# Context FFN in three passes with its own banks beside the later quarters, and a modulation on VectorE that the scheduler may place

## The chip, the cores and the metric

The kernel runs on one core of one Trainium2 chip. The metric is the device time of one execution in microseconds (us), taken over several runs. Profiles show one execution each: TensorE appears as PE (its weight loads as PEld), VectorE as DVE, ScalarE as ACT, GpSimd as POOL, SyncE, which issues nearly all DMAs, as SP.

## What is computed

Two blocks follow each other on 256 tokens of width 1024, all in float32. The first block has a layer with a token mix (a bidirectional RWKV-7 recurrence beside a Hyena long convolution), a convolved FFN and a gated embedding, and a layer with neighbourhood attention. The second block is a two-layer network over two streams, `x` and a context `ctx`, whose norms are modulated by vectors made from `c` and `c_ctx`. What matters here is that the first half FFN of the context in the second block does not depend on the first block at all:

```
z   = rmsnorm(x, mix_norm) @ mix_w_in                      # 3328 columns
x   = x + concat(rwkv7_bidir(z[:1664]), hyena_bidir(z[1664:])) @ mix_w_out
x   = x + conv_ffn(x) ; x = x + ple(x) ; x = x + na(x) ; ...
...
mc  = split(silu(c_ctx) @ w_mod[0] + b_mod[0], 9)           # and ml from c
ctx = ctx + 0.5 * mc[2] * swiglu(rms_norm(ctx, g) * (1 + mc[1]) + mc[0], wg, wu, wd)   # D_FF = 2816
```

## The kernel before

Activations lie feature by feature: 8 tiles of 128 features by 256 tokens. Weights come from memory as tiles of 128 rows by up to 1024 columns, one DMA each. The exact products are made in one of two ways. `plain` (L397) gives TensorE the float32 tiles as they are; the trace shows two records for each such product. `gemm` (L368) first splits both operands into a rounded high part and a rest, with a cast on ScalarE (L362) and a subtraction on VectorE or GpSimd (L363), and then runs three passes, high by high, high by rest, rest by high (L371 to L373).

The program is written as one sequence, and a scheduler then sets the order of each engine's instructions for good. It may move an instruction of one part ahead of another part unless the instruction is pinned with `keep_in_program_order`, or the buffers do not allow it: a tile can only be written when the last user of its buffer is done. Each engine then works through its list in order, and so does SP with the DMAs.

`mix` (L839) is the first layer's token mix. The recurrence is cut into four quarters of two heads each (`Recurrence.prepare`, L1587, and `Recurrence.solve`, L1663). A quarter prepares its operands (products L1606, sums, exponentials, many VectorE steps), forms a triangular system (L1678), inverts it in six levels (products L1705, each followed by VectorE steps L1719, L1724, L1725), walks through four chunks (L1739, L1743, L1750), and writes its output (L1769 to L1782). Nothing in a quarter's chain can be reordered, so the scheduler puts other TensorE work between its steps: the projections by `w_in0` (`project`), the Hyena filters and the convolution (`filters`, `hyena`), the output product (`out0`), and the context's work. Quarters use the PSUM tags `a` and `b` in turn, three banks each, and all other work shares the two banks of tag `fill`.

The context's work in `mix` has three parts. `mod_first` (L1019) makes 24 modulation tiles for layer 0 on TensorE: 48 products of two columns by 512 (L1030), with transposes behind them. `norm_ctx` (L956) norms the context. `ctx_ffn` (L967) then runs the FFN in eight groups of three hidden tiles (`FILL`); its first four groups (`CUT`) run in `mix` by `plain` (up products L400 from `xc`, down products L1006), the others later by `gemm` in the gaps of the next layers, in the pool `own`, with GpSimd doing the subtractions.

PSUM is one pool per stage. The pool of `mix` closes at its end, and the next stage (`conv_ffn` of layer 0, here ffn0) opens another one with tags `mm`, `aux` and `fill`; without the pool option `reuse_waits="tile"` the new pool waits for the old one as a whole. Weights of `plain` land in the pool `wha` (tags `wh` and `wl`, two buffers each) through `room` (L392).

Later modulation tiles are made by `mod_until` (L1054): for each tile a DMA of 512 KB, and on VectorE a multiplication with the broadcast vector and a sum (L1077), one per stream or one with help of GpSimd (`aid`), all pinned to the program's order.

Of the kernel before, what the change touches and what calls it, by code (L numbers as in the profile page):

```python
# [153 lines left out]
def layout(inp):  # L154
# [17 lines left out]
    for l in range(2):  # L172
# [30 lines left out]
    a["ccf"] = np.ascontiguousarray(a["cc"].reshape(2, KT, P).transpose(2, 1, 0))  # L203
    a["w_modk"] = np.ascontiguousarray(
        g["w_mod_2"][0][:, :3072].reshape(4, 2, P, 6, 512).transpose(3, 0, 2, 1, 4).reshape(24, P, 1024))
# [70 lines left out]
class Net:  # L276
# [98 lines left out]
    def plain_tiles(self, name, todo):  # L375

        arr = self.ap[name]
        i = 0
        while i < len(todo):
            t, k0, kn = todo[i]  # L380
            n = kn * P
            m = 1
            while i + m < len(todo) and (m + 1) * n <= 1024 and todo[i + m] == (t + m, k0, kn):
                m += 1
            raw = self.room()
            src = arr[t : t + m, :, k0 * P : k0 * P + n].rearrange("t p n -> p t n")
            self.nc.sync.dma_start(raw[:, : m * n].rearrange("p (t n) -> p t n", t=m), src)
            for j in range(m):
                yield t + j, raw[:, j * n : (j + 1) * n]
            i += m  # L390

    def room(self):  # L392

        self.whi += 1
        return self.t(self.wha, [P, 1024], ("wh", "wl")[self.whi % 2])

    def plain(self, out, w, kt, x):  # L397

        for k in range(kt):
            self.nc.tensor.matmul(out, w[:, k * P : (k + 1) * P], x[:, k], start=k == 0, stop=k == kt - 1)  # L400
# [89 lines left out]
    def sq_add(self, m, s=0):  # L490

        nc = self.nc
        x = self.t(self.nrm, [P, T], f"ss{s}", bufs=1) if m == 0 else self.t(self.nrm, [P, T], "xt")
# [6 lines left out]
        else:  # L500
            self.sl[s].append(x)

# [8 lines left out]
    def norm1(self, pool, gname, tag="xn"):  # L511
# [5 lines left out]
        for k in range(KT):  # L517
            x = self.t(self.nrm, [P, T], "xt")
# [320 lines left out]
    def mix(self, ef):  # L839
# [4 lines left out]
        with ExitStack() as es:  # L844
            pool = self.pool(es, "mix")
            y = self.t(pool, [P, 4, T], "y")
            cs = self.t(pool, [P, KT, 2], "cs")
            nc.sync.dma_start(cs, self.ap["ccf"])
            self.tc.keep_in_program_order(nc.scalar.activation(cs, cs, AF.Silu))
            xp = self.pool(ef, "xc", side="right")  # L850
            xc = Parts([self.t(xp, [P, T], "xc", bufs=KT + 1) for _ in range(KT)])
            fp = self.pool(es, "fill", side="right")
            with ExitStack() as e2:
# [7 lines left out]
                with ExitStack() as e3:  # L861
# [3 lines left out]
                    with ExitStack() as e4:  # L865
# [6 lines left out]
                        self.tag = self.aux = "fill"  # L872
# [38 lines left out]
                        with ExitStack() as e5:  # L911
                            yp = self.pool(e5, "hyf")
                            self.tag = self.aux = "fill"
# [3 lines left out]
                            self.tag = self.aux = "fill"  # L917
# [5 lines left out]
                        project([7, 3, 11])  # L923
                        self.tag = self.aux = "fill"
                        self.mod_first(pool, cs)
                        self.norm_ctx(xc)
                        project([14 + 4 * j + q for q in range(4) for j in range(3)])
                    for j in range(2, 4):
                        solve(j, prepare(j))
                        if j == 2:  # L930
                            self.tag = self.aux = "fill"
                            self.hyena(x0, sv, kr, ki, hn)
                self.tag = self.aux = "fill"
# [5 lines left out]
        fp = self.pool(ef, "fill2", side="right")  # L939
        xh, xl = self.t(fp, [P, KT, T], "xnh", F32R), []  # L940
        for k in range(KT):
# [861 lines left out]
```

## Time and profile before

| what | value |
|---|---|
| three runs, median (lowest to highest) | 2967.49 us (2966.17 to 2968.52) |
| profiled execution, its own time | 2961.21 us |
| its span | 2959.4 us |
| granted TensorE clock, mean over the span | 0.964 |
| busy: PE, PEld, DVE, ACT, POOL | 96%, 83%, 63%, 40%, 13% |
| first product of ffn0 (L409) | 604.54 us after the start |

A matmul's record is drawn from its start to its modelled end and overlaps the next ones, so a busy TensorE can be one that waits between short products. What a product costs in a row of equal ones is the step from one start to the next. A line of the code can be a helper's, so a group is known by its line and its tiles together.

### The profile page before, as it was taken

How to read it: one execution, taken by the hardware profiler on the slowest of the kernel's cores; microseconds unless marked ns; L12 is line 12 of the kernel's file. 1: busy time of each engine (PE TensorE's matmuls, PEld its weight loads, DVE VectorE, ACT ScalarE, POOL GpSimd, SP SyncE). 2: the span in 40 equal slices, each digit the busy share in tenths (PEclk: the TensorE clock that was granted, in tenths of full speed). 3: DMA queues.
4: the chain of work that ended last, by engine and by line, in shares of the span. 5: the costliest groups of instructions: out<-in, count | busy, mean ns of one | idle time of the engine just before them, and what ended most of it. 6: DMA issues, size and time to landing. Idle time of an engine off the chain costs nothing.

```text
span 2959.4 us, 48347 instructions
## 1 busy us (share of the span) xinstructions
PE 2834.2 (96%) x19346; PEld 2452.0 (83%) x19346; DVE 1877.3 (63%) x3408; ACT 1175.0 (40%) x2065; POOL 385.9 (13%) x254
## 2 busy tenths in 40 slices
PE   7999999999989989988999999999999999999999
PEld 5756777889989889988998758888888888896899
DVE  5424632288977768886773584777765555558555
ACT  3202200065555545555554463322233222355443
POOL 0000000032252421122220101000010000102100
PEclk7998988999999999999999999999999999999999
DMA  4142123466545536645751203555544444221464
GB/s 133 51 144 95 52 80 119 130 226 206 199 166 168 148 115 215 212 147 197 227 179 57 91 1 107 171 178 178 170 150 130 152 132 144 91 92 57 148 194 150
DMA packets 146914, 414.81 MB, mean 140 GB/s; under 512 B 31153, under 2 KB 51266, under 8 KB 145922
## 3 DMA queue, kind: packets, MB, share of 16 engines
q1 hardware_dynamic: 145970, 406.48, 42.9%
q0 software_dynamic: 720, 5.24, 0.4%
q8 instruction: 153, 2.51, 0.3%
q14 instruction: 71, 0.58, 0.1%
HBM read 410.62 MB, written 1.05 MB: 139 GB/s over the span
## 4 chain that ended last, share of the span: by engine, by line
PE 79%; DVE 12%; issue 4%; ACT 2%; DMA 2%; POOL 0%; SPq 0%; DVEq 0%; ACTq 0%; POOLq 0%
PE mm L372 17%; PE mm L373 17%; PE mm L371 17%; PE fill L400 7%; DVE wl L363 3%; PE mm L1458 2%; PE mm L410 2%; PE mm L411 2%; PE mm L409 1%; PE fill L1030 1%; PE mm L1426 1%; PE fill L1006 1%; PE a L1705 1%; ACT wh L362 1%; PE aux L462 1%
## 5 line engine op out<-in xcount | busy, mean ns | idle before, releaser
L362 ACT CAST wh<-raw 128x1024 fp32r<-128x1024 f32 (+4 forms) x596 | 565.5, 957 | 953.7 <-PE mm L372 549.2
L363 DVE TENSOR_TENSOR wl<-raw,wh 128x1024 fp32r<-128x1024 f32 (+3 forms) x524 | 661.3, 1266 | 296.4 <-ACT wh L362 276.8
L371 PE MATMUL mm<-xnh,wh 128*128 128x256 f32 (+1 forms) x2592 | 818.1, 316 | 4.2 <-ACT u L527 3.2
L373 PE MATMUL mm<-xnh,wl 128*128 128x256 f32 (+1 forms) x2592 | 818.6, 316 | 2.1 <-DVE wl L363 2.1
L372 PE MATMUL mm<-xnl,wh 128*128 128x256 f32 (+1 forms) x2592 | 818.4, 316 | 0.4 <-DVE xnl L363 0.2
L371 PEld LDWEIGHTS mm<-xnh,wh 128*128 128x128 f32 x2592 | 489.0, 189 | 41.7 <-ACT u L527 3.4
L373 PEld LDWEIGHTS mm<-xnh,wl 128*128 128x128 f32 x2592 | 489.3, 189 | 35.2 <-DVE wl L363 3.1
L372 PEld LDWEIGHTS mm<-xnl,wh 128*128 128x128 f32 x2592 | 489.1, 189 | 33.9 <-DVE xnl L363 1.0
L372 PE MATMUL mm<-ml,wh 128*128 128x256 f32 (+1 forms) x1104 | 342.2, 312 | 10.8 <-DVE ml L363 10.8
L371 PE MATMUL mm<-mh,wh 128*128 128x256 f32 (+1 forms) x1104 | 338.8, 313 | 5.3 <-ACT mh L362 2.4
L373 PE MATMUL mm<-mh,wl 128*128 128x256 f32 (+1 forms) x1104 | 340.4, 311 | 0.0
L1077 DVE CUSTOM_DVE_ANT_0 junk<-wm,sc,vecs 128x1024 bf16<-128x1024 f32 x200 | 257.0, 1285 | 5.6 <-DMA wm<-w_mod 1.9
L372 PEld LDWEIGHTS mm<-ml,wh 128*128 128x128 f32 x1104 | 208.8, 189 | 24.8 <-DVE ml L363 12.2
L371 PEld LDWEIGHTS mm<-mh,wh 128*128 128x128 f32 x1104 | 206.1, 189 | 20.5 <-ACT mh L362 3.2
L373 PEld LDWEIGHTS mm<-mh,wl 128*128 128x128 f32 x1104 | 208.3, 189 | 12.0
L363 POOL TENSOR_TENSOR wl<-raw,wh 128x1024 fp32r<-128x1024 f32 (+2 forms) x72 | 135.2, 1886 | 626.8 <-ACT wh L362 610.2
L499 POOL TENSOR_TENSOR ss<-ss,xt 128x256 f32<-128x256 f32 x56 | 59.0, 1060 | 887.0 <-issue 688.9
L1081 POOL TENSOR_TENSOR wm<-wm,sc 128x1024 f32<-128x1024 f32 x40 | 109.9, 2747 | 437.2 <-DVE mod L1077 354.3
L410 PE MATMUL mm<-xnl,wh 128*128 128x256 f32 x416 | 123.6, 303 | 11.6 <-DVE xnl L363 6.2
L1199 DVE TENSOR_TENSOR sg<-sg,mm 128x256 f32<-128x256 f32 (+1 forms) x88 | 48.7, 554 | 121.6 <-PE mm L373 119.3
L1152 DVE SCALAR_TENSOR_TENSOR H<-mm,mod,H 128x256 f32<-128x256 f32 x112 | 53.8, 482 | 113.2 <-PE mm L373 112.9
L411 PE MATMUL mm<-xnh,wl 128*128 128x256 f32 x416 | 121.7, 298 | 2.0 <-DVE wl L363 2.0
(552 smaller groups left out, 4205.1 us busy)
## 6 DMA issues: line engine op xcount, KB each, us to landing
raw<-s_up SPq DMA_DIRECT2D x196, 512.0 KB, 4.2
wm<-w_mod SPq DMA_DIRECT2D x120, 512.0 KB, 4.4
raw<-f_up SPq DMA_DIRECT2D x88, 512.0 KB, 4.4
raw<-s_dn SPq DMA_DIRECT2D x65, 512.0 KB, 3.6
raw<-w_in SPq DMA_DIRECT2D x34, 512.0 KB, 3.7
raw<-s_dn SPq DMA_DIRECT2D x44, 384.0 KB, 3.1
raw<-f_dn SPq DMA_DIRECT2D x32, 512.0 KB, 4.1
raw<-w_qkv SPq DMA_DIRECT2D x24, 512.0 KB, 3.7
```

What stands on the lines that cost most here:

```text
L362: self.nc.scalar.copy(hi, src)
L363: (self.nc.gpsimd if pool or self.own and self.tag == "fill" else self.nc.vector).tensor_sub(lo, src, hi.bitcast(F32))
L371: nc.tensor.matmul(out, wh[:, ws], h, start=first and k == 0, stop=False)
L372: nc.tensor.matmul(out, wh[:, ws], l, start=False, stop=False)
L373: nc.tensor.matmul(out, wl[:, ws], h, start=False, stop=last and k == kt - 1)
L400: self.nc.tensor.matmul(out, w[:, k * P : (k + 1) * P], x[:, k], start=k == 0, stop=k == kt - 1)
L410: nc.tensor.matmul(out, wh[:, s], l, start=False, stop=False)
L411: nc.tensor.matmul(out, wl[:, s], h, start=False, stop=k == kt - 1)
L499: (nc.gpsimd if self.tag == "mm" else nc.vector).tensor_add(self.ss[s], self.ss[s], x)
L1077: self.tc.keep_in_program_order(nc.vector.tensor_tensor_reduce(out=junk, in0=w, in1=self.sc[:, i], scale=0.5 if self.half else 1.0, scalar ...
L1081: nc.gpsimd.tensor_mul(w, w, self.sc[:, 1])
L1458: nc.tensor.matmul(po[64 * h : 64 * h + 64, :T], v(k0 // P + i), pTs[h][:, i], start=i == 0, stop=i == nk // P - 1)
```

## The change

- `ctx_ffn` runs all its groups by `gemm`, in three passes, with the operands of `norm2`; the first four groups still come in `mix`, and 13 up tiles instead of 12. `norm_ctx`, `room` and the second splitting of `xc` are gone. Weights are split into the pool `wha` (two buffers each of `wh` and `wl`); they land in a pool `raw` with two buffers that is opened in the room that the Hyena part leaves.
- PSUM in `mix` has four tags of two banks: `a`, `b`, `in` for the mix's own products and `fill` for the context. A chunk step of `solve` takes one bank in three column ranges where it took three banks. The PSUM pool gets `reuse_waits="tile"`, so a bank passes on when its own last user is done.
- The 24 modulation tiles are made by `mod_until` on VectorE, two sums per tile, weights in `wha`, DMAs and sums not pinned. `mod_first` is gone, and with it the layouts `ccf` and `w_modk`. The broadcast `sc` (1024 KB) is loaded by SP in place of `cs`.
- Weights of `plain` land in a pool `whole` with four buffers of 512 columns, so a tile of 1024 columns takes two DMAs.
- `hyena` stands behind the second quarter and the projections, ahead of quarters 2 and 3 (counted from 0).

```diff
-        self.psum = es.enter_context(self.tc.tile_pool(name=self.nm("psum"), bufs=1, space=PSUM))
+        self.psum = es.enter_context(self.tc.tile_pool(name=self.nm("psum"), bufs=1, space=PSUM, reuse_waits="tile"))
...
+            self.mod_open(pool, aid=False, eng=nc.sync, room=self.wha)
+            self.whole = self.pool(es, "whole", bufs=4)
...
+                        self.mod_until(0)
...
-                        project([7, 3, 11])
-                        self.tag = self.aux = "fill"
-                        self.mod_first(pool, cs)
-                        self.norm_ctx(xc)
-                        project([14 + 4 * j + q for q in range(4) for j in range(3)])
-                    for j in range(2, 4):
-                        solve(j, prepare(j))
-                        if j == 2:
-                            self.tag = self.aux = "fill"
-                            self.hyena(x0, sv, kr, ki, hn)
-                self.tag = self.aux = "fill"
+                        project([7, 3, 11] + [14 + 4 * j + q for q in range(4) for j in range(3)])
+                    self.tag = self.aux = "in"
+                    self.hyena(x0, sv, kr, ki, hn)
+
+                fp = self.pool(ef, "fill", side="right")
+                self.raw = self.pool(es, "raw", bufs=2, side="right")
+                for j in range(2, 4):
+                    solve(j, prepare(j))
+                self.tag = self.aux = "in"
                 self.out0(0, 3, y)
                 self.out0(3, 1, y[:, 3:], True)
-                for _ in self.ctx_ffn(fp, FILL[:CUT], xc):
-                    pass
+                self.tag = self.aux = "fill"
+                self.mod_until(12)
+                self.rest = self.ctx_ffn(fp)
+                for _ in range(CUT):
+                    next(self.rest)
...
+        keep = (lambda ins: ins) if self.modw else self.tc.keep_in_program_order
...
+                if self.modw:
+                    w = self.t(self.modw, [P, D], ("wh", "wl")[j])
...
-                self.nrm = self.pool(e2, "nrm", bufs=3)
+                self.nrm = self.pool(e2, "nrm", bufs=2)
-                self.psum_open(e2, a=3, b=3, fill=2)
+                self.psum_open(e2, a=2, b=2, **{"in": 2}, fill=2)
...
-            psr, psu, pss = net.acc("aux"), net.acc("aux"), net.acc("aux")
+            bank = net.acc("aux")
+            psr, psu, pss = (bank[:, i * P : (i + 1) * P] for i in range(3))
```

How the scheduler's lists change is seen at three places. The first is VectorE in the preparation of quarter 0, soon after the projections begin; `c`, `tot` and the `rs...b` tiles belong to that quarter. Before:

```order
L1614 COPY tot_290<-c_258 128x8
L1616 TENSOR_TENSOR c_258<-lw_257,c_258 128x256
L1617 TENSOR_TENSOR c_258<-c_258,tot_290 128x256
L1583 SCALAR_TENSOR_TENSOR v_261<-zs_112,vecs_58,v_261 128x256 x2
L1620 TENSOR_TENSOR lw_257<-c_258,lw_257 128x512
L1609 TENSOR_SCALAR a_256<-a_256 128x512
L429 TENSOR_SCALAR rsxb_308<-b_303 128x8
L434 TENSOR_SCALAR rsyb_309<-rsxb_308 128x8
```

With the change:

```order
L1568 COPY tot_287<-c_255 128x8
L496 TENSOR_TENSOR ss_603_3427<-ss_603_3427,xtfill_3432 128x256
L431 TENSOR_SCALAR rsyb_306<-rsxb_305 128x8
L1031 ISA junk_3299,mod_73<-wl_3297,sc_92,vecs_58 128x1024
L1031 ISA mod_73 128x1
L1570 TENSOR_TENSOR c_255<-lw_254,c_255 128x256
L496 TENSOR_TENSOR ss_603_3427<-ss_603_3427,xtfill_3435 128x256
L433 TENSOR_TENSOR rshb_307<-rsxb_305,rsyb_306 128x8
L1031 ISA junk_3301,mod_73<-wl_3297,sc_92,vecs_58 128x1024
```

L1031 is the modulation's sum (L1077 before). One such pair stands between almost any two steps of the chains, and all 48 stand ahead of the third level of quarter 0's inversion.

The second place is TensorE in the inversion of quarter 2 (tag `b`; 16 products L1705, L1659 with the change, form one half of a level). Before:

```order
L1705 MATMUL b_2325<-xyt_2194,G_2146 64x64 x16
L1705 MATMUL b_2343<-xyt_2194 64x64 x16
L1705 MATMUL b_2360<-xyt_2194 64x64 x16
L831 MATMUL fill_2660<-c_dfti_2625,st_2648 128x256 x2
L831 MATMUL fill_2660<-c_dfti_2625,kr_921 128x256 x2
L1705 MATMUL b_2379<-xyt_2194,G_2146 64x64 x16
```

With the change:

```order
L1659 MATMUL b_2335<-xyt_2186 64x64 x16
L1659 MATMUL b_2352<-xyt_2186 64x64 x16
L369 MATMUL fill_3505<-xnl_3450,wh_3508 128x256
L370 MATMUL fill_3505<-xnh_3449,wl_3509 128x256
L368 MATMUL fill_3505<-xnh_3449,wh_3508 128x256
L369 MATMUL fill_3505<-xnl_3450,wh_3508 128x256
L370 MATMUL fill_3505<-xnh_3449,wl_3509 128x256
L368 MATMUL fill_3505<-xnh_3449,wh_3508 128x256
L1659 MATMUL b_2371<-xyt_2186,G_2138 64x64 x16
```

The Hyena products between the levels have gone ahead, and up products of the context FFN stand in their place.

The third place is TensorE where quarter 3 ends (its last product is L1779, L1734 with the change). Before, the rows behind it are out0's last step and then the whole context FFN of the first four groups, 576 records; `fill_3460` is its first up tile:

```order
L1779 MATMUL a_3358<-gd_113,gup_2890 128x256
L400 MATMUL fill_3414<-y_91,wl_3412 128x256
L400 MATMUL fill_3419<-y_91,wl_3412 128x256
...
L400 MATMUL fill_3460<-xc_98,wh_3461 128x256
```

With the change `fill_4472` is a down product of the second of the four groups that is already under way:

```order
L1734 MATMUL a_3168<-gd_101,gup_2708 128x256
L368 MATMUL fill_4472<-mh_4112,wh_4468 128x256
L369 MATMUL fill_4472<-ml_4113,wh_4468 128x256
L370 MATMUL fill_4472<-mh_4112,wl_4469 128x256
```

From quarter 2's first inversion product to this place TensorE's list has 633 three-pass products of the context, from here to ffn0's sums another 280, and 35 up to ffn0's first product. From that product on the two lists are equal.

## Rows read from the trace of the kernel before

**Rows 1.** The page's first two parts: busy time, and the span in 40 slices.
```profile
PE 2834.2 (96%) x19346; PEld 2452.0 (83%) x19346; DVE 1877.3 (63%) x3408; ACT 1175.0 (40%) x2065; POOL 385.9 (13%) x254
...
PEclk7998988999999999999999999999999999999999
```

**Rows 2.** Windows by stage; columns as in the head line, PEclk is the granted clock.
```profile
core 0: us, PE busy (x) PEld busy (x) DVE busy (x) ACT busy (x) POOL busy (x), PEclk, DMA share, GB/s
0.00:20.00 20.00, 10.53 (x39) 9.11 (x40) 8.45 (x32) 3.97 (x9) 0.20 (x4) 1.00 0.88 256
20.00:113.00 93.00, 80.39 (x586) 58.54 (x586) 58.91 (x142) 33.34 (x67) 2.35 (x1) 0.76 0.20 68
...
113.00:293.00 180.00, 176.00 (x1463) 112.15 (x1462) 62.62 (x162) 36.76 (x78) 0.00 (x0) 0.92 0.32 107
293.00:421.00 128.00, 122.56 (x1463) 96.15 (x1465) 69.93 (x164) 20.54 (x41) 4.69 (x2) 0.97 0.22 68
421.00:458.00 37.00, 28.52 (x220) 20.06 (x216) 9.04 (x31) 3.06 (x8) 0.72 (x1) 0.67 0.20 72
458.00:592.00 134.00, 132.49 (x592) 113.23 (x592) 30.96 (x72) 10.36 (x28) 0.00 (x0) 0.98 0.43 130
592.00:604.50 12.50, 10.72 (x84) 10.26 (x85) 10.39 (x26) 7.35 (x12) 5.45 (x3) 1.00 0.71 248
604.50:1310.00 705.50, 661.70 (x5249) 635.45 (x5247) 583.20 (x978) 392.82 (x707) 216.85 (x119) 0.97 0.55 179
```

**Rows 3.** Chain of waits in order of time, two pieces of 458 to 592 us (start, us, what).
```profile
465.02 27.91 PE fill L400 x128
494.30 9.33 PE fill L1006 x42
```

**Rows 4.** Timeline of TensorE: plain products, 13 equal records, then the next row.
```profile
465.77 2.97 PE L400 MATMUL fill<-xc,wh 128*128 128x256 f32 x13
468.58 1.67 PE L400 MATMUL fill<-xc,wl 128*128 128x256 f32 x7
```

**Rows 5.** Timeline of TensorE: three-pass products, first and 55th record of a dense row.
```profile
759.76 0.28 PE L371 MATMUL mm<-mh,wh 128*128 128x256 f32 x1
...
766.12 0.28 PE L371 MATMUL mm<-mh,wh 128*128 128x256 f32 x1
```

**Rows 6.** Groups of TensorE, 0 to 620 us: context FFN and modulation (busy us, mean ns).
```profile
L400 PE MATMUL fill<-xc,wh 128*128 128x256 f32 x192 | 43.5, 380 | 0.1
...
L1030 PE MATMUL fill<-wl,cs 128*2 128x512 f32 x48 | 23.3, 608 | 0.0
L1006 PE MATMUL fill<-mh,wh 128*128 128x256 f32 x96 | 23.1, 384 | 0.8 <-DVE mh L991 0.5
```

**Rows 7.** Timeline of TensorE: the modulation's products.
```profile
157.20 1.88 PE L1030 MATMUL fill<-wl,cs 128*2 128x512 f32 x4
158.91 1.88 PE L1030 MATMUL fill<-wh,cs 128*2 128x512 f32 x4
```

**Rows 8.** Line L1077, the modulation's sum on VectorE (ns minimum, median, maximum).
```profile
L1077 DVE CUSTOM_DVE_ANT_0 junk<-wm,sc,vecs x200: 1270/1280/2039, 651.1 to 2548.7; 128x1024 bf16<-128x1024 f32 x100
L1077 DVE DVE_READ_ACCUMULATOR2_ANT mod<- x200: 74/84/90, 652.3 to 2549.9; 128x1 f32 x100
```

**Rows 9.** Timeline of VectorE: third level of quarter 0's inversion.
```profile
111.60 0.69 DVE L1724 TENSOR_TENSOR xyt<-xyt,b 128x512 f32<-128x512 f32 x1 [0.29 <-PE b L1705]
```

**Rows 10.** Chain of waits: the context's load.
```profile
19.16 7.30 DMA Hc<-ctx
```

**Rows 11.** DMA issues, 0 to 620 us (count, KB each, median us to landing).
```profile
wl<-w_modk SPq DMA_DIRECT2D x12, 512.0 KB, 3.5
...
wl<-s_up SPq DMA_DIRECT2D x12, 512.0 KB, 3.5
```

**Rows 12.** Groups of TensorE, 293 to 458 us: projections and a Hyena product.
```profile
L400 PE MATMUL fill<-xn,wh 128*128 128x256 f32 x48 | 11.3, 386 | 0.0
...
L810 PE MATMUL fill<-st,c_dftf 128*128 128x256 f32 x32 | 7.7, 388 | 0.6 <-DMA c_dftf<-dftf 0.6
L400 PE MATMUL fill<-xn,wl 128*128 128x256 f32 x32 | 7.4, 385 | 0.0
```

**Rows 13.** Groups of 1900 to 2200 us: splitting a weight tile.
```profile
L363 DVE TENSOR_TENSOR wl<-raw,wh 128x1024 fp32r<-128x1024 f32 x45 | 55.0, 1223 | 12.5 <-ACT wh L362 10.6
L362 ACT CAST wh<-raw 128x1024 fp32r<-128x1024 f32 x45 | 47.2, 1049 | 184.8 <-PE mm L372 133.5 <-issue 47.1 <-PE mm L373 4.2
```

**Rows 14.** Timeline of TensorE: ffn0's first product.
```profile
604.54 0.40 PE L409 MATMUL mm<-xnh,wh 128*128 128x256 f32 x2
```

More of the change, by code (lines that the diff above doesn't have):

```diff
@@ L501, in sq_add, with xt @@
             self.sl[s].append(x)
+    def xt(self):
+        return self.t(self.nrm, [P, T], "xt" if self.tag == "mm" else "xt" + self.tag)
     def root(self, s=0):
@@ L953, in out0, with ctx_ffn @@
                 self.sq_add(m)
-    def norm_ctx(self, xn):
+    def ctx_ffn(self, pool):
         nc = self.nc
@@ L961, in norm_ctx @@
             self.sq_add(k, 1)
-        r = self.h_rstd(1)
-        for k in range(KT):
-            nc.vector.scalar_tensor_tensor(xn[:, k], self.HH[1][:, k], self.mod[:, 0, 8 + k, 1:2], r, op0=ALU.mult, op1=ALU.mult)
-            nc.scalar.activation(xn[:, k], xn[:, k], AF.Identity, bias=self.mod[:, 0, k, 1:2])
-    def ctx_ffn(self, pool, groups, *x):
-        nc = self.nc
-        whole = len(x) == 1
-        g0, g1 = groups[0][0], sum(groups[-1])
-        tiles = self.plain_tiles if whole else self.pieces
-        it = tiles("s_up00", [(t, 0, KT) for t in range(2 * g0, 2 * g1)])
-        nm = groups[0][1] + 1
+        x = self.norm2(pool, 0, 0, [1])
+        it = self.wtiles("s_up00", range(2 * FT), KT)
         mids = []
@@ L981, in up, with mod_open @@
             for o in pp:
-                _, *w = next(it)
-                if whole:
-                    self.plain(o, *w, KT, *x)
-                else:
-                    self.gemm(o, *w, KT, *x)
+                _, wh, wl = next(it)
+                self.gemm(o, wh, wl, KT, *x)
             s = self.t(pool, [P, T], "sg", bufs=2)
-            m = [self.t(pool, [P, T], "mh", bufs=nm)] if whole else [self.t(pool, [P, T], n, F32R, bufs=nm) for n in ("mh", "ml")]
             nc.scalar.activation(s, pp[0], AF.Tanh, scale=0.5)
             nc.vector.scalar_tensor_tensor(s, s, 1.0, pp[0], op0=ALU.add, op1=ALU.mult)
-            nc.vector.scalar_tensor_tensor(m[0] if whole else s, s, 0.5, pp[1], op0=ALU.mult, op1=ALU.mult)
-            if not whole:
-                self.split(s, *m)
+            nc.vector.scalar_tensor_tensor(s, s, 0.5, pp[1], op0=ALU.mult, op1=ALU.mult)
+            m = [self.t(pool, [P, T], n, F32R, bufs=FILL[0][1] + 1) for n in ("mh", "ml")]
+            self.split(s, *m)
             mids.append([a.unsqueeze(1) for a in m])
-        for k0, kn in groups:
-            yield
-            while len(mids) < min(k0 + kn + 1, g1) - g0:
+        for k0, kn in FILL:
+            while len(mids) < min(k0 + kn + 1, FT):
                 up()
-            for m, *w in tiles("s_dn00", [(m, k0, kn) for m in range(KT)]):
+            for m, wh, wl in self.pieces("s_dn00", [(m, k0, kn) for m in range(KT)]):
                 ps = self.acc()
                 for k in range(kn):
-                    ends = dict(start=k == 0, stop=k == kn - 1)
-                    if whole:
-                        nc.tensor.matmul(ps[:, :T], w[0][:, k * P : (k + 1) * P], mids[k0 - g0 + k][0][:, 0], **ends)
-                    else:
-                        self.gemm(ps[:, :T], *w, 1, *mids[k0 - g0 + k], w0=k, first=k == 0, last=k == kn - 1)
+                    self.gemm(ps[:, :T], wh, wl, 1, *mids[k0 + k], w0=k, first=k == 0, last=k == kn - 1)
                 self.gated(0, 0, m, ps, [1])
-    def mod_open(self, pool, half=False, aid=True, eng=None):
+            yield
+    def mod_open(self, pool, half=False, aid=True, eng=None, room=None):
         nc, cc = self.nc, self.ap["cc"]
@@ L1017, in mod_open @@
         (eng or nc.gpsimd).dma_start(self.sc, bass.AP(tensor=cc.tensor, offset=cc.offset, ap=[[0, P], [D, 2], [1, D]]))
[L1018 to L1040 removed]
+        self.sc_raw, self.half, self.aid, self.modw = True, half, aid, room
     def mod_ends(self, l, s):
@@ L1056, in mod_until @@
         nc = self.nc
-        if self.mod_at < until and self.sc_raw:
+        if (self.mod_at < until or until == 0) and self.sc_raw:
             self.sc_raw = False
@@ L1097, in norm2 @@
             for k in range(KT):
[L1098 removed]
+                x = self.xt()
                 sc = self.mod[:, l, (3 * j + 1) * 8 + k, s : s + 1]
```

77 lines of the change are left out of this document (21 added, 56 removed).

## The prediction

> **What bounds the kernel now.** I read the page's busy shares and slices first [rows 1]: TensorE is busy 96% of the span, the next engine 63%, so TensorE's list is where time can be won. The slices show where its clock falls: in the first slice, and again around the sixth and seventh. Because both kernels have the same TensorE list from ffn0's first product on, which stands at 604.54 us [rows 14], I leave the 2355 us behind it alone and ask only how much earlier that product comes. The windows by stage [rows 2] say what limits each part ahead of it. From 20 to 113 us (up to the third level of quarter 0's inversion, [rows 9]) TensorE's mean clock is 0.76 and VectorE is idle for 34 of 93 us: a chain of small steps with projections between them. From 421 to 458, in quarter 3, TensorE has 28.5 us of work in 37 at clock 0.67: too little to put between the steps. From 458 to 592 it is full for 132.5 of 134 us, and the chain of waits has nothing there but TensorE's own context products [rows 3]. That last stretch is what the change goes for.
>
> **The change, term by term.** Prices: a plain product is two records, and 13 records from 465.77 to 468.58 make 0.216 us each, 0.43 a product [rows 4]; three passes step by (766.12 − 759.76)/54 = 0.118, 0.353 a product [rows 5]. The four groups have 576 plain records [rows 6], 124.4 us (the two groups shown there with `wh`, 192 and 96 records, have twins with `wl`); with one more up tile they become 913 three-pass instructions, 107.5 us.
>
> *20 to 113 us, the modulation.* 48 sums come to VectorE at 1.28 us, with a read of 0.08 that partly overlaps [rows 8]; I take 1.30, so 62 us. By the order all stand ahead of quarter 0's third level. VectorE has 58.9 busy us there [rows 2], so from about 25 us, when the first weight lands behind the initial loads (the context's load has the wait chain until 26 us, [rows 10], and goes behind), it needs 121 us: the level comes at 146, with small waits 150 instead of 112 (**+37**). Least is +31, if the first weight comes at 20; most +62, if no sum falls into the 34 idle us. The loads should not stop it: 24 weights in 125 us are one per 5.2 us, and such a load takes 3.5 from issue to landing [rows 11].
>
> TensorE's 80.4 us of work there, done at 0.76, would fit under 125 us even at 0.5 (80.4 × 0.76/0.5 = 122), if only just; I take it as covered. The Trainium skill ("TensorE: Matmul & The Clock Gate", section "Part 1: The HAM clock gate") speaks against that: "the default state is throttled, and activity releases the throttle", so an engine that waits for VectorE more would stay at 1.2 GHz. The trace agrees so far that its two thinly filled stretches are those at 0.76 and 0.67; which level a stretch bound by VectorE gets, no row shows. It is the third rival below.
>
> *113 to 293 us.* 96 modulation products leave TensorE: four records take 1.71 us [rows 7], 0.428 each, 41 us. In come 80 projection records (80 × 0.216 = 17 us) that now stand between 293 and 458 [rows 12], and about half of Hyena's products, 7 us (32 of them and their twins, 7.7 us busy, same rows). That is 24 back, 17 less in all, and I add 3 for waits that go with them (176 busy of 180 at 0.92 [rows 2] leaves 18 us of such waits): **−20**. Ends: −35 (the late front takes projections that then no longer stand here) and 0 (the quarters' chains set this stretch anyway).
>
> *293 to 458 us, quarters 2 and 3.* 633 three-pass instructions come in, 75 us; the 24 us above leave. Nothing hidden is +51, everything hidden 0. What hides them is TensorE's own waits in the quarters' chains, seen as idle time or as a low clock: from 421 to 458 they are worth 37 − 28.5 × 0.67 = 18 us at full clock, from 293 to 421 128 − 122.6 × 0.97 = 9 [rows 2]. A product is not always at hand when its gap comes, so of these 27 us I take 16 as hidden: **+35**. More than 27 can be hidden only if records drawn as busy hold waits, which between short products they can.
>
> *458 to 592 us.* 280 instructions are left (33 us) and out0's last step (3.5). They are fed by two raw buffers: landing 3.5 [rows 11], cast 1.05, subtraction 1.22 [rows 13], 5.8 us per tile, with two buffers one per 2.9 us, against 24 × 0.118 = 2.83 us of products: level, a little worse for the narrow down pieces. 45 us instead of 134: **−89** (−97 with no wait; −82 with 52 us).
>
> *592 to 604.5 us.* 35 context products stand ahead of ffn0's first product instead of 78, and the sums of ffn0's norm can start with the bank-wise release instead of the whole pool's: 43 × 0.118 = 5, and 2 of wait: **−7** (−10 to 0).
>
> What I cost at nothing: two DMAs per projection tile (the DMA share is 0.2 to 0.3 up to 458 us), two banks for `a` and `b` and one per chunk step (a third product of a level waits for a VectorE step that the level needs anyway; cover: the VectorE-bound front, else some us per quarter, within the ends of the two stages from 113 to 458 us), 26 casts of 1.05 and 32 short ones on ScalarE at 40% busy, subtractions of 26 × 1.22 us on VectorE, which is busy 142 of the 345 us from 113 to 458 [rows 2].
>
> Sum: +37 − 20 + 35 − 89 − 7 = **−44**. The profiled execution took 2961.2 us (span 2959.4), 6.3 below the median; I forecast 2917 for such a one, and against the median 2967.5 − 44 = **2923.5 us**. A check from the other side: work that leaves TensorE ahead of ffn0 is 41 + 17 (124.4 − 107.5) + 5 = 63 us; the sum gives back 19 of it to the slow front. More than 63 needs idle time filled.
>
> **Rivals.**
> *1, slower: the front waits for weights.* VectorE works in list order, so a step of quarter 0 stands behind a sum whose weight hasn't landed, and on SP the projections' loads stand behind a load that waits for one of two buffers. With a load of L us from a free buffer to landing, a weight takes (L + 2.7)/2: nothing is lost up to L = 7.7, the whole gain at 24 × 2.1 us more, L = 12; at L = 14, 24 × 8.35 = 200 us, the level at 225, 75 late: +31, **2998**. For it: the context's load waits 7.3 us at the start [rows 10], DMA moves 256 GB/s there. Against: 68 GB/s from 20 to 113 [rows 2], 3.5 us to landing [rows 11].
> *2: the fill doesn't go between.* The order puts the three-pass products between the quarters' steps, but each then delays the step behind it, and the middle gives nothing: +37 + 0 + 51 − 82 − 7 = −1, **2966** (to 2952). For it: before 421 TensorE had 9 us to spare in 128. This is also how the change would fail to do what it says; that the products stayed behind the quarters, its order excludes.
> *3: the low clock.* At 1.2 GHz through the front TensorE's 122 us and VectorE's 125 both lie in one chain, and part of each is seen: I add 20 us. −24, **2943.5**. For it the 0.76 with less waiting than there will be; against it, that big projections are still there to fill.
> *4: it hides better.* The front at +31, the middle at −30 and +15, the end −92 and −8: −84, **2883.5**. For it: in the front TensorE's waits are worth 93 − 80.4 × 0.76 = 32 us, and projections can move into a longer front.
>
> **How the numbers follow.** Forecast (−30 to −60) 0.50; rival 1 0.13; rival 2 0.13, of which 0.05 within 0.2% (6 us, about what a measurement of this kernel can tell from no change) and 0.08 better; rival 3 0.12; rival 4 0.12. Faster 0.50 + 0.08 + 0.12 + 0.12 = 0.82, same 0.05, slower 0.13. The range from 2880 (rival 4's middle; the ends of the terms don't all fall together) to 2967 (rival 2 whole) leaves out rival 1 and half of rival 4, 0.19.
>
> **What would show it.** Right: sums back to back on VectorE from 25 to 150 us; quarter 0's third level near 150; quarter 2's inversion near 310; quarter 3 ending near 510; ffn0's first product near 560. Wrong: VectorE waiting in the front for DMAs of the modulation's weights (rival 1); TensorE idle or stretched out between 310 and 510 (rival 2); a granted clock near 0.5 up to 150 (rival 3); quarter 3 over before 490 (rival 4); or ffn0's first product moved by something other than the total, which would mean that the equal lists behind it don't run equally.

## The result and the profile after

The change makes the kernel faster: 2923.49 us (median of 4 runs, 2920.73 to 2926.44) against 2967.82, ratio 0.9852, 95% interval 0.9835 to 0.9869. The forecast was 2923.5. Its total is right; four of its five terms are within 11 us of the trace and one is 18 off, and they cancel. The profiled execution's span went from 2959.4 to 2919.0 us, 40.4 less where the medians differ by 44.3, so the agreement to the last digit is luck.

The page after, busy times and granted clock, beside [rows 1]:

```profile
PE 2785.4 (95%) x19514; PEld 2456.0 (84%) x19514; DVE 1975.3 (68%) x3569; ACT 1216.6 (42%) x2119; POOL 382.8 (13%) x251
...
PEclk7798999999999999989999999999999999999999
```

Windows of the changed kernel at the same points of the program as [rows 2]: quarter 0's third inversion level, quarter 2's first inversion product, quarter 3's end, the sums of ffn0's norm, ffn0's first product, the end (columns as there):

```profile
20.00:143.30 123.30, 92.37 (x588) 64.62 (x589) 109.39 (x241) 34.28 (x68) 3.21 (x1) 0.72 0.44 150
143.30:293.30 150.00, 146.04 (x1406) 117.14 (x1401) 77.07 (x176) 35.12 (x72) 0.00 (x0) 0.92 0.23 72
293.30:511.70 218.40, 212.95 (x2247) 182.80 (x2247) 118.94 (x263) 56.66 (x103) 0.72 (x1) 0.93 0.27 87
511.70:553.90 42.20, 39.29 (x298) 37.17 (x297) 30.21 (x62) 19.09 (x36) 0.00 (x0) 1.00 0.49 156
553.90:565.50 11.60, 6.22 (x35) 6.01 (x34) 10.03 (x21) 6.26 (x11) 6.53 (x3) 0.60 0.71 272
565.50:2919.00 2353.50, 2278.24 (x14917) 2039.39 (x14915) 1621.20 (x2780) 1059.51 (x1825) 372.10 (x243) 0.98 0.47 150
```

| stretch | before, us | after, us | forecast | measured |
|---|---|---|---|---|
| up to quarter 0's third level | ends 111.6 | ends 143.3 | +37 | +31.7 |
| to quarter 2's inversion | 181.0 | 150.0 | −20 | −31.0 |
| quarters 2 and 3 | 165.4 | 218.4 | +35 | +53.0 |
| tail, up to the norm's sums | 134.1 | 42.2 | −89 | −91.9 |
| norm, up to ffn0's first product | 12.4 | 11.6 | −7 | −0.8 |
| ffn0's first product | at 604.5 | at 565.5 | −44 | −39.0 |
| from there on | 2354.9 | 2353.5 | 0 | −1.4 |

The equal lists behind ffn0's first product do run equally. The two terms that miss by most, −31.0 and +53.0, share a boundary that has moved: the last 54 products of quarter 1 (L1724), which stood ahead of quarter 2's first inversion product, now stand behind it (294.9 to 302.1 us). A later point is safer: the second subtraction L1678 (L1724 before) in quarter 2's inversion, ahead of which no kernel here has a product of the context FFN. Here it is in the kernel before, the change, e1, e2 and e3, in this order (the last three are told below; the same statement has another line number in each):

```profile
329.70 0.69 DVE L1724 TENSOR_TENSOR xyt<-xyt,b 128x512 f32<-128x512 f32 x1
344.13 0.68 DVE L1678 TENSOR_TENSOR xyt<-xyt,b 128x512 f32<-128x512 f32 x1
308.34 0.69 DVE L1679 TENSOR_TENSOR xyt<-xyt,b 128x512 f32<-128x512 f32 x1
327.50 0.69 DVE L1708 TENSOR_TENSOR xyt<-xyt,b 128x512 f32<-128x512 f32 x1
343.16 0.68 DVE L1680 TENSOR_TENSOR xyt<-xyt,b 128x512 f32<-128x512 f32 x1
```

With the boundary there, all that stands ahead is +14.4 us (+37 − 20 = +17 forecast) and the rest of quarters 2 and 3 is +39.3 (+35 forecast). Windows on both sides of it, before and with the change:

```profile
292.60:329.70 37.10, 36.47 (x337) 28.99 (x338) 20.19 (x55) 10.46 (x21) 0.00 (x0) 1.00 0.36 116
329.70:458.00 128.30, 115.02 (x1348) 87.55 (x1342) 58.78 (x141) 13.49 (x28) 5.41 (x3) 0.88 0.17 55
...
293.30:344.10 50.80, 47.42 (x377) 36.36 (x378) 17.66 (x44) 7.92 (x15) 0.00 (x0) 0.87 0.23 76
344.10:511.70 167.60, 165.53 (x1878) 146.44 (x1875) 101.27 (x220) 48.74 (x88) 0.72 (x1) 0.95 0.29 91
```

In the front the steps show where they were looked for. VectorE's timeline in quarter 0's preparation has a sum between almost any two steps of the chain, with no idle time (start, us, what):

```profile
58.50 0.68 DVE L1585 TENSOR_TENSOR ar<-kk,lw 128x512 f32<-128x512 f32 x1
59.10 1.27 DVE L1031 CUSTOM_DVE_ANT_0 junk<-wh,sc,vecs 128x1024 bf16<-128x1024 f32 x1
60.30 0.08 DVE L1031 DVE_READ_ACCUMULATOR2_ANT mod<- 128x1 f32 x1
60.30 0.15 DVE L436 TENSOR_TENSOR rsafill<-rsafill,rshfill 128x2 f32<-128x2 f32 x1
60.38 0.28 DVE L746 TENSOR_SCALAR hy<-hy 64x256 f32<-64x256 f32 x1
60.58 0.68 DVE L1587 TENSOR_TENSOR kk<-kk,a 128x512 f32<-128x512 f32 x1
61.18 1.27 DVE L1031 CUSTOM_DVE_ANT_0 junk<-wh,sc,vecs 128x1024 bf16<-128x1024 f32 x1
...
143.27 0.68 DVE L1678 TENSOR_TENSOR xyt<-xyt,b 128x512 f32<-128x512 f32 x1
```

The last row answers to [rows 9]: quarter 0's third level. VectorE's waits from 24 to 132 us (line waited for, us in total, times, longest) name a weight's DMA once:

```profile
DVE junk L1031 <- DMA wh<-w_mod: 3.1, 1, 3.1
```

Line L1031, beside [rows 8], has the sums at the same price as before's later ones, from 23.7 to 131.5 us:

```profile
L1031 DVE DVE_READ_ACCUMULATOR2_ANT mod<- x48: 70/77/84, 24.9 to 131.5; 128x1 f32 x48
L1031 DVE CUSTOM_DVE_ANT_0 junk<-wh,sc,vecs x24: 1264/1272/1285, 23.7 to 127.6; 128x1024 bf16<-128x1024 f32 x24
```

The same total could come from parts that were each wrong, so the experiments price the parts: the sums, their place, the place of the FFN, and the three passes. In each, theory A and rival B are those of the text that was on record before the run. All ratios are to the kernel before on the same chip; the change stands at 0.9852.

### The profile page after: what moved, and what is told of

It is laid out like the page before. It is cut to its first block, busy times and chain, and to the rows that moved or that the text cites. A ratio compares the mean times of both kernels' runs of the same rounds, so it can differ in the third digit from the quotient of the medians.

```text
span 2919.0 us, 49031 instructions
## 1 busy us (share of the span) xinstructions
PE 2785.4 (95%) x19514; PEld 2456.0 (84%) x19514; DVE 1975.3 (68%) x3569; ACT 1216.6 (42%) x2119; POOL 382.8 (13%) x251
## 4 chain that ended last, share of the span: by engine, by line
PE 79%; DVE 13%; issue 4%; ACT 2%; DMA 2%; POOL 0%; SPq 0%; ACTq 0%; DVEq 0%; POOLq 0%
PE mm L370 17%; PE mm L368 17%; PE mm L369 17%; PE in L397 4%; DVE wl L360 3%; PE mm L1412 2%; PE fill L370 2%; PE fill L368 2%; PE fill L369 2%; PE mm L407 2%; DVE junk L1031 2%; PE mm L408 2%; PE mm L406 2%; PE mm L1380 1%; PE a L1659 1%
## 5 line engine op out<-in xcount | busy, mean ns | idle before, releaser
L359 ACT CAST wh<-raw 128x1024 fp32r<-128x1024 f32 (+3 forms) x652 | 607.0, 938 | 1026.8 <-PE mm L369 556.3
L360 DVE TENSOR_TENSOR wl<-raw,wh 128x1024 fp32r<-128x1024 f32 (+3 forms) x582 | 711.3, 1226 | 316.4 <-ACT wh L359 307.2
L1031 DVE CUSTOM_DVE_ANT_0 junk<-wm,sc,vecs 128x1024 bf16<-128x1024 f32 x200 | 256.7, 1284 | 5.5 <-DMA wm<-w_mod 1.9
L370 PEld LDWEIGHTS mm<-mh,wl 128*128 128x128 f32 x1104 | 208.6, 190 | 12.4
```

What stands on the lines that cost most here:

```text
L359: self.nc.scalar.copy(hi, src)
L360: (self.nc.gpsimd if pool or self.own and self.tag == "fill" else self.nc.vector).tensor_sub(lo, src, hi.bitcast(F32))
L370: nc.tensor.matmul(out, wl[:, ws], h, start=False, stop=last and k == kt - 1)
L1031: keep(nc.vector.tensor_tensor_reduce(out=junk, in0=w, in1=self.sc[:, i], scale=0.5 if self.half else 1.0, scalar=self.vecs[:, b + t : b + ...
```

## Experiments

**e1, the sums cut short.**

```diff
-   out=junk, in0=w, in1=self.sc[:, i], scale=...
+   out=junk[:, :64], in0=w[:, :64], in1=self.sc[:, i, :64], scale=...
```

> Edit: the 48 modulation sums in the mix run over 64 of 1024 columns (the other columns are left out of the sums); loads, instruction count and everything else as in the changed kernel. About 57 us of VectorE time leave the front. Theory A (the front's delay is repaid, because TensorE's total work from the start to the end of quarter 1 sets the time): quarter 0's third level comes some 25 us earlier, but the first product of quarter 2's inversion and of ffn0 hardly move: 2915 to 2923 us. Rival B (the 32 us by which quarter 0 is late are paid in full): 2890 to 2898 us.

2887.7 us, ratio 0.9742 (0.9719 to 0.9765): the time that leaves VectorE costs about 1.1%, 33 us. A sum still takes 0.28 us instead of 1.27, so 48 us leave, not the 57 expected. ffn0's first product shows it, the change first:

```profile
L406 PE MATMUL mm<-xnh,wh x32: 276/280/415, 565.5 to 579.5; 128*128 128x256 f32 x32
```

and e1:

```profile
L406 PE MATMUL mm<-xnh,wh x32: 278/279/284, 530.6 to 544.2; 128*128 128x256 f32 x32
```

Theory B holds: the 34.9 us between the two starts are paid. On the way some is given back and lost again: e1 has quarter 0's third level at 102.5 us, 40.8 earlier than the change, quarter 2's first inversion product at 267.6, 25.7 earlier, and the second L1678 step of that inversion (L1679 in e1) at 308.3, 35.8 earlier.

**e2, the modulation back on TensorE.**

```diff
-            self.mod_open(pool, aid=False, eng=nc.sync, room=self.wha)
+            cs = self.t(pool, [P, KT, 2], "cs")
...
-                        project([7, 3, 11] + [14 + 4 * j + q for q in range(4) for j in range(3)])
+                        project([7, 3, 11])
+                        self.tag = self.aux = "fill"
+                        self.mod_first(pool, cs)
+                        project([14 + 4 * j + q for q in range(4) for j in range(3)])
```

> Edit: the changed kernel with the modulation of before: 48 products of 512 columns back on TensorE, their transposes and copies, no sums on VectorE in the mix. Theory A (TensorE's work sets the front): 41 us of products come back and nothing is won from the freed VectorE but part of the waits: +25 to +41, 2948 to 2964 us. Rival B (the modulation's 62 us on VectorE cost 32): -32 + 41 and fewer waits, 2923 to 2935 us.

2902.3 us, 0.9794 (0.9771 to 0.9817). This was outside both: the change without its modulation part is 0.6% faster than the change, 17 us by the ratios. Windows of e2, the front and quarters 2 and 3:

```profile
20.00:92.40 72.40, 72.34 (x292) 36.85 (x290) 41.24 (x107) 36.29 (x70) 0.00 (x0) 1.00 0.60 206
...
296.20:484.00 187.80, 185.16 (x2104) 160.63 (x2103) 113.30 (x251) 51.60 (x91) 0.72 (x1) 0.96 0.30 96
```

At quarter 2's first inversion product the two places for the modulation seem to cost the same (296.2 us against 293.3), but there e2 has quarter 1's last 54 products behind it and the change has not. At the second L1678 step of the inversion (L1708 in e2) e2 is 16.6 us ahead, 327.5 against 344.1, with no product of the context FFN done in either; that is the whole difference at ffn0 (549.2 against 565.5). Behind that step the rest of the quarters takes 156.5 us with 553 of the FFN's products and 167.6 with 633 in the change, and the tail, with the 80 that are left for it, is 12.5 longer in e2.

**e3, the FFN behind the quarters.**

```diff
         x = self.norm2(pool, 0, 0, [1])
+        nc.vector.scalar_tensor_tensor(x[0][:, 0, :1], self.gate[:, 3, :1], 0.0, x[0][:, 0, :1].bitcast(F32), op0=ALU.mult, op1=ALU.add)
```

> Edit: the first product of the context FFN takes an operand that waits for quarter 3's output, so that all 913 three-pass products of the four groups stand behind the quarters, as the plain ones did before. Theory A (nothing is hidden beside quarters 2 and 3: those 633 products cost their 75 us there): the quarters become 55 us shorter, the stretch behind them 75 to 80 longer, ffn0 comes at 565 to 590: 2923 to 2948 us. If the quarters' own chains were at their limit before (165 us with or without the Hyena products that have left), the upper end; if they shrink by the 24 us that left, the lower. Rival B (the fill beside the quarters is the source of the gain): the quarters' stretch stays as long as it was before, 165 us, and the tail grows by more than 90 because two raw buffers can't feed it: over 2955 us.

2959.9 us, 0.9986 (0.9974 to 0.9998): nearly the whole gain is gone. Windows of quarters 2 and 3, and of the tail:

```profile
292.60:458.00 165.40, 143.00 (x1614) 111.36 (x1614) 72.76 (x182) 21.55 (x47) 0.72 (x1) 0.79 0.12 40
458.00:592.60 134.60, 122.12 (x930) 115.56 (x929) 80.58 (x144) 54.10 (x92) 0.81 (x1) 0.98 0.45 141
```

The quarters take 165.4 us, to a tenth what they took before, although 80 projection records and 32 records of Hyena products have left them. The equality is a sum of two changes, as windows of e3 on both sides of the second L1678 step (L1680 in e3) show beside those of before:

```profile
292.60:343.20 50.60, 47.22 (x379) 36.28 (x380) 17.69 (x45) 7.87 (x15) 0.00 (x0) 0.87 0.23 76
343.20:458.00 114.80, 95.78 (x1243) 75.08 (x1238) 55.06 (x139) 13.68 (x32) 0.72 (x1) 0.75 0.08 24
```

Behind the step 112 records of plain products have left (64 of out0, 48 of Hyena), 24 us at 0.216 each, and the time is 13.5 us shorter, with the steps of the context's norm on VectorE added there. Ahead of it there are 96 such records in both (80 of the projections and 16 of Hyena before, 64 of out0 and 32 of Hyena in e3), but quarter 1's last 54 products have come in (7 us), the granted clock is 0.87 instead of 1.00, and the time is 13.5 us longer. So in sum the work that left was worth nothing; where it left it gave back a good half. What the lower clock and the order each cost ahead of the step was not separated.

e3 and the change agree up to that step (50.6 and 50.8 us into the stretch). The 633 products behind it cost 218.4 − 165.4 = 53 us, 0.084 each, 71% of their 0.118. Behind the quarters the same products cost 134.6 − 42.2 = 92 us. The 37 us between ffn0's starts (602.9 and 565.5) are what the placing beside the quarters brings; three passes in the old place bring nothing (134.6 us of tail against 134.1).

**e4, the FFN plain beside the quarters.**

```diff
-                _, wh, wl = next(it)
-                self.gemm(o, wh, wl, KT, *x)
+                self.plain(o, *next(itp)[1:], KT, x[0].bitcast(F32))
```

> Edit: the first four groups of the context FFN beside the quarters run as plain float32 products (two records each) with the weights taken as they land, no casts and no subtractions; the low part of the normed context is left out of their up products. TensorE gets 22 us more work, VectorE and ScalarE lose about 26 subtractions of 1.22 us with 32 short ones, and as many casts. Theory A (TensorE's work sets the quarters' stretch): +15 to +25, 2938 to 2948 us. Rival B (the quarters are slowed by the subtractions that stand in VectorE's list between their steps): at most +5, and down to -15: 2908 to 2928 us.

2935.6 us, 0.9906 (0.9880 to 0.9931), 16 us over the change by the ratios, theory A by its total. But only 6 of them stand ahead of ffn0 (571.5), at the edge of what theory B allowed; the rest lies behind it, where the lists are no longer those of the change, and was not followed. Beside the quarters 464 plain records make the stretch 235.2 us, 69.8 more than e3's 165.4: 0.150 each, 70% of [rows 4]'s 0.216. So a product beside the quarters shows seven tenths of its own time in either form.

**e5, the subtractions on GpSimd.**

```diff
-        (self.nc.gpsimd if pool or self.own and self.tag == "fill" else ...
+        (self.nc.gpsimd if pool or self.tag == "fill" else ...
```

> Edit: in the mix the context FFN's subtractions (38 of a whole weight tile in the quarters' stretch, and 13 of a hidden tile) go to GpSimd instead of VectorE; the order then has 482 of the 913 products ahead of quarter 3's end, not 633. In the changed kernel 633 products made that stretch 53 us longer (0.085 us each, of 0.118). Theory A (TensorE's own order: a product that has begun stands ahead of the quarter's step): the same 0.085 each, 41 us, quarters 2 and 3 take 206 us; the tail gets 151 more products at 0.147, +22: about 10 us slower than the change, 2934 us. Rival B (the subtractions on VectorE hold the quarters' steps up): at most 0.04 each, 185 us, and the sum 8 to 15 us faster than the change, 2908 to 2915 us.

2946.0 us, 0.9931 (0.9904 to 0.9957): worse than both expected. The quarters take 215.6 us with 482 products, and the tail 71.7 instead of 42.2, where TensorE's longest waits are for GpSimd's subtractions (6.6 us in 10 waits). It doesn't separate the theories, since GpSimd takes longer for a subtraction (mean 1.79 us up to 620 us, narrow pieces included, against VectorE's 1.00 in the change) and gets in VectorE's way, as e6 shows. e9 asks the question better.

**e6, GpSimd helps with the sums.**

```diff
-            self.mod_open(pool, aid=False, eng=nc.sync, room=self.wha)
+            self.mod_open(pool, aid=True, eng=nc.sync, room=self.wha)
```

> Edit: the modulation's second sum per tile is made by GpSimd (product, 2.75 us) and ScalarE (sum) instead of VectorE, in the form that the later modulation tiles already have. VectorE keeps 24 sums, 31 us, and gets 24 small additions. Theory A (VectorE's 62 us in the front are the loss of about 17 us against the modulation on TensorE, and 33 us against none): about half of the 33 comes back, 2905 to 2912 us. Rival B (24 weights held in two buffers each for 2.75 + 1.3 us more hold up the chain, or ScalarE's list does): 2920 to 2935 us.

2960.3 us, 0.9990 (0.9979 to 1.0000): VectorE has half the sums, and the front is 40 us slower than in the change (quarter 0's first inversion product at 138.8 us instead of 99.2). Neither theory has the cause; the timelines of GpSimd and VectorE do:

```profile
49.46 2.49 POOL L1035 TENSOR_TENSOR wl<-wl,sc 128x1024 f32<-128x1024 f32 x1 [1.35 <-DVE rsyb L431]
53.18 2.54 POOL L1035 TENSOR_TENSOR wh<-wh,sc 128x1024 f32<-128x1024 f32 x1 [1.23 <-ACT wl L1036]
...
49.66 3.37 DVE L1031 CUSTOM_DVE_ANT_0 junk<-wh,sc,vecs 128x1024 bf16<-128x1024 f32 x1
53.44 2.56 DVE L496 TENSOR_TENSOR ss<-ss,xtfill 128x256 f32<-128x256 f32 x1
```

A sum of 1.27 us that begins 0.2 us after a GpSimd product lasts 3.37 and ends 1.08 after it; an addition of 0.41 us lasts 2.56 and ends 0.28 after the next. From 20 to 300 us, 23 of VectorE's instructions take over 1.5 times their median in the change, 45.8 us more in all. That outweighs the sums saved: ahead of quarter 0's first inversion product VectorE has 24 sums in e6 and 32 in the change.

**e7, the sums behind quarter 0's preparation.**

```diff
                         ready = prepare(0)
+                        for i in range(2):
+                            nc.vector.scalar_tensor_tensor(self.sc[:, i, :1], ready[3][:, :1], 0.0, self.sc[:, i, :1], op0=ALU.mult, op1=ALU.add)
```

> Edit: the sums wait for the end of quarter 0's preparation (two small operations write back the broadcast vectors after it), so that they stand among the inversions, where VectorE is less than half busy, and not in the preparation, where it was the bound. Theory A (the place of the sums in the preparation is what costs): quarter 0's first inversion product comes near 67 us instead of 99, and most of the 17 us that the move of the modulation costs come back: 2903 to 2912 us. Rival B (wherever they stand ahead of the fill, 62 us in VectorE's list hold up one chain or another by the same amount): 2918 to 2930 us.

2899.6 us, 0.9786 (0.9767 to 0.9805): theory A, 20 us faster than the change by the ratios. Windows of e7 up to quarter 0's inversion and up to quarter 1's:

```profile
20.00:64.90 44.90, 39.13 (x160) 28.66 (x158) 33.02 (x87) 23.95 (x49) 0.00 (x0) 0.75 0.42 154
64.90:173.60 108.70, 97.11 (x858) 74.97 (x858) 98.02 (x200) 21.95 (x44) 3.20 (x1) 0.87 0.44 141
```

The inversion begins at 64.9 us, 99.2 in the change. The sums now fill VectorE from 57 to 152 us, yet ffn0 comes at 541.5, 10.9 later than with the short sums of e1, against 34.9 in the change. Among the inversions the sums cost a third of what they cost in the preparation.

**e8, the bank-by-bank release alone, in the kernel before.**

```diff
-tile_pool(name=self.nm("psum"), bufs=1, space=PSUM)
+tile_pool(name=self.nm("psum"), bufs=1, space=PSUM, reuse_waits="tile")
```

> Edit: the kernel before with nothing but the bank-by-bank release of PSUM between stages. The prediction gave this and 43 fewer products 7 us at the start of ffn0; the changed kernel showed 1. Theory A: nothing that can be told from zero, ratio 0.998 to 1.002, 2959 to 2971 us. Rival B (every stage's start gains by it, hidden in the change by the two raw buffers): 5 to 15 us faster.

2963.4 us, 1.0003 (0.9991 to 1.0015): nothing. What TensorE waits for at ffn0's start in the change is the norm itself:

```profile
PE aux L480 <- DVE rsyaux L441: 5.4, 1, 5.4
```

**e9, no subtractions beside the quarters.**

```diff
-                self.split(raw[...], hi[:, :n], lo[:, :n], ...)
+                nc.scalar.copy(hi[:, :n], raw[...])
+                lo = hi
```

> Edit: in the mix the context FFN's weight tiles are only cast; the third pass takes the cast tile again in place of the rest, so the weights' low part and the 38 subtractions on VectorE in the quarters' stretch (34 us busy) are left out. TensorE's products stay three per step; 587 of them stand ahead of quarter 3's end, 633 in the changed kernel. Theory A (TensorE's order sets that stretch: what begins stands ahead of the quarter's step): quarters 2 and 3 as long per product as in the change, 165 + 587 x 0.085 = 215 us, ffn0 within 5 us of the change: 2918 to 2928 us. Rival B (the subtractions in VectorE's list hold the quarters' steps): 180 to 195 us for the two quarters, 2893 to 2908 us.

2920.1 us, 0.9848 (0.9829 to 0.9867), no difference from the change. Window of quarters 2 and 3:

```profile
296.00:505.20 209.20, 204.71 (x2201) 175.18 (x2201) 87.91 (x222) 54.75 (x99) 0.72 (x1) 0.93 0.30 89
```

VectorE is 31 us less busy than in the change (87.9 against 118.9), and 587 products still cost 209.2 − 165.4 = 44 us, 0.075 each instead of 0.084. So the weights' subtractions explain some 5 us of this stretch; most of its cost is TensorE's own list. (ffn0 comes 5.7 us earlier, at 559.8, and the rest takes 8 longer, which was not followed.) The casts on ScalarE stay in e9, so it says nothing on them.

**e10, e7 with three groups in the mix** (`CUT = 3`; e12 has `CUT = 2`).

> Edit: the kernel with the sums behind quarter 0's preparation, and three instead of four groups of the context FFN in the mix; the fourth runs with the later ones between the next layers' products. Some 235 products leave the stretch behind quarter 3, about 33 us at the pace of that stretch in the change (274 in 42 us, with out0's last step). Theory A (those layers leave TensorE full, 96% busy, so each product costs at least its 0.118 us there too): within 6 us of the kernel with four, 2894 to 2906 us. Rival B (they have gaps in which a product is hidden): down to 2875 us.

2878.8 us, 0.9712 (0.9697 to 0.9727): theory B, the fastest kernel here, 1.4% below the change by the ratios. Windows of its tail and norm, and of all behind ffn0's first product:

```profile
482.80:499.40 16.60, 16.51 (x122) 15.59 (x121) 14.00 (x37) 9.24 (x21) 0.00 (x0) 1.00 0.45 135
499.40:510.60 11.20, 6.14 (x36) 5.94 (x35) 9.64 (x20) 5.87 (x11) 6.45 (x3) 0.70 0.74 282
...
510.60:2876.70 2366.10, 2293.31 (x15133) 2055.46 (x15131) 1637.85 (x2794) 1070.42 (x1845) 403.48 (x260) 0.98 0.48 151
```

The 216 products that left were worth 30.9 us ahead of ffn0 (510.6 against e7's 541.5) and cost 10.8 behind it (2366.1 against 2355.3): 0.05 each of their 0.118.

**e11, e7 with three raw buffers** (`"raw", bufs=3`).

> Edit: the kernel with the sums behind quarter 0's preparation, and three instead of two buffers in which the context FFN's weights land. Theory A (two buffers hold up the stretch behind quarter 3: 42 us for 36 us of products): 3 to 6 us less there, 2894 to 2897 us. Rival B (the waits there are for sums and casts, not for room): no difference that can be told, 2896 to 2903 us.

2902.1 us, 0.9793 (0.9776 to 0.9809): theory B, nothing that can be told from e7.

**e12, e7 with two groups.**

> Edit: the kernel with the sums behind quarter 0's preparation, and two groups of the context FFN in the mix. With three groups the 216 products that left the stretch ahead of ffn0 made it 31 us shorter (ffn0 at 510.6 instead of 541.5) and the rest 11 us longer. With two, the order has 165 fewer ahead of ffn0, 114 of them beside the quarters. Theory A (beside the quarters a product costs 0.085 us, so these give back less than behind them, 114 x 0.085 + 51 x 0.14 = 17 us, and the later layers have few gaps left, 165 x 0.118 = 19): no difference from three groups, 2875 to 2885 us. Rival B (the later gaps hide half of them as they did): 2865 to 2873 us.

2895.5 us, 0.9783 (0.9767 to 0.9800): slower than three groups, outside both. ffn0 comes 12.5 us earlier than in e10 (498.1), 17 or more were expected; the rest takes 28.5 longer (2394.6 against 2366.1), 0.17 for each of 165 products. That is more than their own 0.118, so something besides TensorE's time is lost there; it was not followed. The later layers had room for one group, not for two.

## Why the prediction was right, step by step

- **The front, +37: right, +31.7.** 48 sums at 1.27 us came where the order put them, VectorE was busy 109.4 of 123.3 us, and the level came at 143 instead of 150. Rival 1 fell: one wait of 3.1 us for a weight. Its price was also too high, since it counts two buffers where the weights use two tags of two in turn; by its own rule with four, (L + 2.7)/4, nothing is lost up to a load of 18 us. Rival 3 did not come: the granted clock of this stretch is 0.72, between its levels of 1.2 and 2.4 GHz, not 0.5.
- **Up to quarter 2's inversion, −20: −31.0, at its end of −35.** Without most of the sums this stretch is 165.1 us long (e1, 102.5 to 267.6), 15.9 shorter than before, 7 of it by quarter 1's last products, which crossed its end. The other 15.1 are time of the late front that is given back at this boundary, which the forecast had only as an end. Little of that lasts: at the second L1678 step of the inversion 35.8 of the 40.8 us that the sums cost are still there. So the sign "near 310" for quarter 2's inversion was missed, at 293.3, and the term was nearly right one step later.
- **Quarters 2 and 3, +35: +53.0, the term that was wrong by most.** It took +75 for the products, −16 for what is hidden and −24 for the projections and Hyena products that leave. The price of the products was near, 53 for 59. The −24 was mis-sized: by e3 the work that left gave back 13.5 behind the second L1678 step. And 13.5 more come ahead of that step, which the term put at nothing: quarter 1's last products are 7 of it, and the granted clock there fell from 1.00 to 0.87. The chain that leaves TensorE waiting makes filler cheap and makes work that leaves it worth less than its own time; the prediction used it for one and not for the other. Rival 2's +51 came near the total of this stretch for another reason, since it had nothing hidden, and 22 of the 75 us were.
- **The tail, −89: right, −91.9.** Two raw buffers do not hold it up (e11, in the kernel of e7).
- **The norm, −7: −0.8.** 5 of it were for 43 fewer context products and 2 for the release of banks. The release alone is worth nothing (e8). TensorE's busy time here fell from 10.7 to 6.2 us and the stretch stayed: VectorE's chain, busy 10.0 of 11.6 us, sets this start.
- **At nothing:** the weights' subtractions were rightly costed near nothing, some 5 us beside the quarters and nothing in the total (e9). The casts, the fewer banks and the doubled DMAs were not tried one by one.

The errors, measured less forecast, are −5, −11, +18, −3 and +6: +5 of −44. The right total is partly luck. With the boundary at the second L1678 step the errors are smaller, −3, +4, −3 and +6, so part of what cancels is only where the line was drawn. What the forecast did not see is that the parts have opposite signs. The FFN beside the quarters brings 37 us at ffn0 (e3 against the change), three passes against plain 6 there and 16 in the runs (e4), and the modulation on VectorE, as placed, loses 16 there and 17 in the runs (e2).

## What to carry to other kernels

Where a latency chain sets a stretch, filler put into it costs a share of its own time (here seven tenths, in either form of product), and work taken out of it gives back a share too (here 13.5 of 24 us behind one step, and nothing over the whole stretch): do not credit work that leaves in full beside filler that hides. Set the boundary between two stretches at a step of the chain, not at a product that the scheduler may move past another. Work given to a less busy engine is judged at the place where it lands: against a kernel with 48 of the 62 us of sums taken out, the whole sums cost 35 us in a preparation that VectorE itself then bounds and 11 behind it, among the inversions. And a part that can go to several stages, like the FFN's groups, is priced in each, since here a group cost 31 us in one and 11 in another.

## What the runs showed of the hardware that was not expected

GpSimd products of two operands held up VectorE instructions, the two shown in e6 until the product had ended, so that halving VectorE's sums with GpSimd's help made VectorE's front longer (23 instructions, 45.8 us, e6). With GpSimd's subtractions in e5 eight instructions were held in quarters 2 and 3, 10.5 us. The Trainium skill has a rule for it ("SBUF — State Buffer", section "Who interferes with whom"): a VectorE instruction with two inputs there contends with a GpSimd instruction that reads there, and the port pair that the two engines share is an exclusive lock. The trace agrees, with 3.37 us for a sum of 1.27; 19 of the 23 have two inputs, and four have one, which this sentence does not cover.

The granted clock of the front went with how busy TensorE was: with the modulation's products on TensorE it was 1.00 from 20 to 92 us, with TensorE busy 72.3 of 72.4 (e2), in the change 0.72, with 92.4 of 123.3, a mean between the levels of 1.2 and 2.4 GHz. The Trainium skill's rule that the prediction cited ("TensorE: Matmul & The Clock Gate", section "Part 1: The HAM clock gate") points the same way. What the lower clock costs in the total was not separated from the sums' own time.
